# A four-layer hybrid decoder trunk: the tile layer orders each engine's instructions by its timeline model

## The chip, the cores and the metric

The kernel runs on one core of a Trainium2 chip. A core has five engines with an instruction stream each: PE (matrix products and transposes), DVE (vector work), ACT (activations and casts), POOL, and SP, which here only issues transfers. Semaphores make an engine wait for another's result; within a stream the order is fixed when the kernel is built. The metric is the device time of one execution in microseconds (us); less is better.

## The reference

A residual stream x of 256 tokens and 1024 features passes four layers in float32. Each layer has a token mixer, a cross-attention to 256 memory tokens and an MLP, and after each of the three a layer norm:

```python
for i in range(DEPTH):                      # DEPTH = 4
    # mixer i mod 3: 0 convolution module, 1 dilated attention, 2 RWKV-7
    x = layer_norm(DEEPNORM_ALPHA * x + mixer(x), ...)
    x = layer_norm(DEEPNORM_ALPHA * x + cross_attention(x, mem), ...)   # 4 heads of 256
    x = layer_norm(DEEPNORM_ALPHA * x + relu(x @ w1) ** 2 @ w2, ...)    # 1024 -> 4096 -> 1024
```

This sketch shortens the reference's code: the layers' mixers are thus convolution, dilated attention, RWKV-7 and convolution again.

## The kernel before

**Tiling.** x lies in SBUF as two tiles of 128 tokens by 1024 features. In the orders shown below they are named x_81 (tokens 0 to 127) and x_82 (tokens 128 to 255); the profile calls both x. A matrix product needs x transposed (features on partitions) and, to keep the precision of float32, in two parts, a rounded high part and the remainder: `xth` and `xtl`. `transposes` (L209, L213) turns four blocks of 128 x 128 on PE into one PSUM tile `psT`, and `split` (L151 to L153) casts it to the high part on ACT and subtracts to the low part on DVE.

**Weights.** Each chunk of 512 KB is loaded raw to `ws` (L137, three buffers), cast by ACT to its high part `wh` (L138) and subtracted by DVE, or POOL in one stretch, to its low part `wl` (L139); `wh` and `wl` have nine buffers each. A product is then three matmuls: high by high, high by low, low by high. `gemm_tok` (L156, matmul at L171) makes a product for one token tile with the 512 columns of a PSUM tile at a time; `gemm_feat` (L183) and `gemm_unit` (L195) make products for all tokens.

**The boundary between two sub-layers.** `project` (L280) runs the output product of a sub-layer for the first token tile, then its norm, then the product for the second tile and its norm. `norm` (L260) adds the product to x (L269) and takes statistics (L270) for each half, aggregates them (L271), works out 1 / sqrt(variance) with single-column steps on DVE (`rsqrt`, L238 to L245), then does a subtraction and scaling (L275) and a second scaling and shift (L276) for each half. Its end writes the transposes of the new x into the next sub-layer's `xth` and `xtl`. The next sub-layer's first product can start on the first token tile as soon as its parts are there. The MLP's first units (`first_rows`, L198) are made for one token tile and then for the other.

**What sets the order.** The mixers' work is interleaved in the program by generators (`merge`, with paces at L43 to L52). But the order in which the program names the operations is not yet that of the engines: the tile layer sorts each engine's instructions by its own model of when they can run, within what the data and the buffers allow, and places the semaphores to fit. With `tile.TileContext(nc)` (in `kernel`) it does so in its default way.

**Stages.** In the profiled execution (us from the start): convolution 0 to 190, cross-attention to 270, MLP to 457; dilated attention 457 to 765, cross-attention to 850, MLP to 1014; RWKV 1014 to 1355, cross-attention to 1445, MLP to 1605; convolution 1605 to 1780, cross-attention to 1862, MLP to 2045, last norm to 2056. The memory's keys and values (`kv_unit`) are made inside the mixers' stretches. In the dilated mixer a query or key unit is 24 matmuls (L648), and each pair of heads has scores, a softmax on DVE and ACT (L727 to L736), transposes of its result (copied at L750) and value products. In the convolution, taps are summed on PE and on DVE (L528); in the RWKV tail ACT copies the scan's parts (L1091).

Of the kernel before, what the change touches and what calls it, by code (L numbers as in the profile page):

```python
# [5 lines left out]

# [4 lines left out]

F32 = mybir.dt.float32
F32R = mybir.dt.float32r
# [11 lines left out]
DEPTH = 4  # L25
# [1271 lines left out]


@with_exitstack
def tile_trunk(ctx: ExitStack, tc: tile.TileContext, t: dict, out: bass.AP, stop: int = 99, layers=tuple(range(DEPTH))):  # L1300
    nc = tc.nc
    k = Trunk(ctx, tc, t)
    for i in range(NT):
        nc.sync.dma_start(k.x[i], t["x"][0, i * P:(i + 1) * P, :])
    xt = k.xt()
    for i in range(NT):
        k.to_xt(xt, k.x[i], i, layers[0] % 3 == 1)
    n = 0
    kv = {}
    done = False  # L1310
    fill = []

    def memory(ls, spare):

        mt = k.mem_t(spare=spare)
        for l in ls:
            kv[l] = k.kv_alloc()
        return [lambda l=l, u=u: k.kv_unit(l, kv[l], u, mt) for l in ls for u in range(8)]

    def staged(l):  # L1320

        mt = k.mem_t(spare=True)
        st = k.dr.tile([8, P, 512], F32, name="kvst")

        def last(us):
            kv[l] = k.kv_alloc()
            k.kv_load(kv[l], [u for u in range(8) if u not in us], st)
            for u in us:
                k.kv_unit(l, kv[l], u, mt)

        return [lambda u=u: k.kv_unit(l, None, u, mt, st) for u in range(8)] + [lambda: last(())]

    for i, layer in enumerate(layers):
        if layer % 3 == 0 and not fill:
            fill = memory((0, 1) if layer == 0 else (layer,), layer > 0)
        elif layer % 3 == 2 and not fill:
            fill = staged(layer)
        for part in ("mix", "xattn", "mlp"):
            if n >= stop:
                break  # L1340
            n += 1
            last = layer == DEPTH - 1 and part == "mlp"
            xo = None if last else k.xt()
            if part == "mix" and layer % 3 == 0:
                k.conv(layer, layer // 3, xt, xo, fill)
                fill = []
            elif part == "mix" and layer % 3 == 1:
                k.dilated(layer, layer // 3, xt, xo)
            elif part == "mix":
                k.rwkv(layer, layer // 3, xt, xo, fill)  # L1350
                fill = []
            elif part == "xattn":
                if layer not in kv:
                    with tc.tile_pool(name="kvp", bufs=1) as kvp:
                        mt = k.mem_t(kvp)
                        kv[layer] = k.kv_alloc()
                        for u in range(8):
                            k.kv_unit(layer, kv[layer], u, mt)
                k.xattn(layer, kv[layer], xt, xo)
            else:  # L1360
                nx = layers[i + 1] if i + 1 < len(layers) else None
                if nx == 3:
                    fill = memory((3,), True)
                elif nx == 2:
                    fill = staged(2)
                k.mlp(layer, xt, xo, nx is not None and nx % 3 == 1)
                for _ in range(2 if nx == 2 else 0):
                    fill.pop(0)()
            xt = xo
    for i in range(NT):  # L1370
        for j in range(2):
            nc.sync.dma_start(out[0, i * P:(i + 1) * P, j * 512:(j + 1) * 512], k.x[i][:, j * 512:(j + 1) * 512])
# [29 lines left out]
```

## Time and profile before

| What | Before |
|---|---|
| Time, median of 3 runs | 2058.87 us (2056.86 to 2062.66) |
| Time of the profiled execution | 2057.95 us |
| Span of the profiled execution, first to last instruction | 2056.2 us |
| Mean granted TensorE clock | 0.972 |
| ACT busy | 996.1 us (48%) |
| Traffic with HBM | 315.67 MB read, 6.88 MB written, 157 GB/s over the span |

A row of the timeline reads: start in us, duration in us, engine, line, operation, output and inputs, shapes, and how many equal instructions stand together. Square brackets hold the engine's idle time ahead of the row and what ended it. In a list of waits, a row names who waited for whom, the sum in us, the number of times, and the longest. In a row of windows stand the stretch, its length, the busy time and number of instructions of PE, PEld, DVE, ACT and POOL, the granted TensorE clock, the busy share of the DMA engines and GB/s.

### The profile page before, as it was taken

What the parts mean: (1) busy time and instruction counts of PE and PEld (TensorE: products, weight loads), DVE (VectorE), ACT (ScalarE), POOL (GpSimd) and SP (SyncE); (2) the same over time, 40 slices, a digit from 0 to 9 for tenths busy, and PEclk for the clock granted to TensorE, in tenths of its full rate; (3) what the DMA queues carried; (4) which work ended last, traced back from release to release, by engine and by line L of the source; (5) the groups of instructions that cost most, each with busy time, mean ns of one, the idle gap of its engine ahead of it and who ended that gap; (6) DMA issues with size and microseconds to landing.
All of it is one profiled execution on the core that took longest, in us unless ns stands there. A gap on an engine that the chain in (4) does not pass through costs nothing.

```text
span 2056.2 us, 33010 instructions
## 1 busy us (share of the span) xinstructions
PE 1944.8 (95%) x13027; PEld 1716.0 (83%) x13027; DVE 1302.7 (63%) x2524; ACT 996.1 (48%) x1551; POOL 264.9 (13%) x160
## 2 busy tenths in 40 slices
PE   7999999998999999999999989989999898999998
PEld 7998779977999977798888777767898787878996
DVE  3986675454555564755575767776554499667544
ACT  4546445543554533555345634333555355545552
POOL 6960000000000000000011312100000663000000
PEclk9999999998999999999999989999999999999999
DMA  7644447656656533576655334344666441445662
GB/s 228 195 154 145 146 147 232 186 163 186 169 147 175 155 117 112 188 221 186 181 160 169 102 103 118 113 138 129 198 199 188 160 144 52 138 139 179 213 188 78
DMA packets 259739, 325.75 MB, mean 158 GB/s; under 512 B 25701, under 2 KB 219965, under 8 KB 259584
## 3 DMA queue, kind: packets, MB, share of 16 engines
q1 hardware_dynamic: 258432, 322.59, 50.8%
q8 instruction: 102, 1.67, 0.3%
q10 hardware_dynamic: 1152, 1.05, 0.2%
q14 instruction: 53, 0.43, 0.1%
HBM read 315.67 MB, written 6.88 MB: 157 GB/s over the span
## 4 chain that ended last, share of the span: by engine, by line
PE 68%; DVE 15%; DMA 6%; ACT 5%; issue 4%; POOL 1%; SPq 0%; DVEq 0%; ACTq 0%; POOLq 0%
PE psA L171 25%; PE psB L183 19%; PE psB L648 7%; PE psB L195 6%; DVE g L528 3%; DVE wl L139 3%; PE psT L213 3%; ACT wh L138 2%; DMA ws<-in_m_w_dram 2%; PE psB L367 2%; POOL wl L139 1%; DMA ws<-in_x_w_out_dram 1%; DVE x L269 1%; DVE bnst L270 1%; DMA ws<-in_x_w_kv_dram 1%
## 5 line engine op out<-in xcount | busy, mean ns | idle before, releaser
L138 ACT CAST wh<-ws 128x1024 fp32r<-128x1024 f32 x546 | 571.4, 1050 | 664.5 <-PE psA L171 167.0
L139 DVE TENSOR_TENSOR wl<-ws,wh 128x1024 fp32r<-128x1024 f32 (+1 forms) x462 | 568.7, 1234 | 421.4 <-ACT wh L138 418.5
L183 PE MATMUL psB<-xth,wh 128*128 128x256 f32 x1280 | 369.1, 289 | 9.4 <-ACT xth L152 3.7
L183 PE MATMUL psB<-xth,wl 128*128 128x256 f32 x1280 | 367.0, 287 | 7.7 <-DVE wl L139 7.7
L183 PE MATMUL psB<-xtl,wh 128*128 128x256 f32 x1280 | 366.6, 286 | 0.0
L183 PEld LDWEIGHTS psB<-xth,wh 128*128 128x128 f32 x1280 | 249.8, 195 | 14.0 <-ACT xth L152 4.1
L139 POOL TENSOR_TENSOR wl<-ws,wh 128x1024 fp32r<-128x1024 f32 x84 | 211.0, 2536 | 380.9 <-ACT wh L138 372.7
L183 PEld LDWEIGHTS psB<-xth,wl 128*128 128x128 f32 x1280 | 249.5, 195 | 8.9 <-DVE wl L139 8.6
L183 PEld LDWEIGHTS psB<-xtl,wh 128*128 128x128 f32 x1280 | 249.7, 195 | 2.3 <-issue 0.2
L171 PE MATMUL psA<-wh,xth 128*128 128x512 f32 x496 | 180.2, 406 | 3.5 <-ACT xth L152 3.0
L171 PE MATMUL psA<-wl,xth 128*128 128x512 f32 x496 | 177.1, 400 | 0.0
L171 PE MATMUL psA<-wh,xtl 128*128 128x512 f32 x496 | 175.9, 399 | 0.0
L171 PE MATMUL psA<-wh,hth 128*128 128x512 f32 x512 | 163.7, 396 | 0.0
L171 PE MATMUL psA<-wh,htl 128*128 128x512 f32 x512 | 163.3, 395 | 0.0
L171 PE MATMUL psA<-wl,hth 128*128 128x512 f32 x512 | 162.3, 393 | 0.0
L528 DVE SCALAR_TENSOR_TENSOR psA<-chp,ccols,psA 128x256 f32<-128x256 f32 x280 | 119.1, 481 | 3.0 <-PE psA L512 0.4
L171 PEld LDWEIGHTS psA<-wh,xth 128*128 128x128 f32 x496 | 94.8, 193 | 25.2 <-ACT xth L152 7.1
L171 PEld LDWEIGHTS psA<-wl,hth 128*128 128x128 f32 x512 | 96.5, 188 | 22.9
L171 PEld LDWEIGHTS psA<-wh,htl 128*128 128x128 f32 x512 | 96.2, 188 | 22.0
L895 POOL MEMSET rH<- 128x512 f32 x1 | 0.5, 528 | 869.6 <-DVE bnst L270 869.6
L171 PEld LDWEIGHTS psA<-wl,xth 128*128 128x128 f32 x496 | 94.9, 192 | 19.0
L171 PEld LDWEIGHTS psA<-wh,xtl 128*128 128x128 f32 x496 | 94.6, 191 | 18.9 <-DVE xtl L153 0.2
(326 smaller groups left out, 3568.2 us busy)
## 6 DMA issues: line engine op xcount, KB each, us to landing
ws<-in_m_w_dram SPq DMA_DIRECT2D x256, 512.0 KB
ws<-in_b_w_qkv_dram SPq DMA_DIRECT2D x72, 512.0 KB
ws<-in_x_w_kv_dram SPq DMA_DIRECT2D x64, 512.0 KB
ws<-in_a_w_in_dram SPq DMA_DIRECT2D x32, 512.0 KB
ws<-in_x_w_q_dram SPq DMA_DIRECT2D x32, 512.0 KB
ws<-in_x_w_out_dram SPq DMA_DIRECT2D x32, 512.0 KB
ws<-in_c_w_rkv_dram SPq DMA_DIRECT2D x24, 512.0 KB
ws<-in_a_w_out_dram SPq DMA_DIRECT2D x16, 512.0 KB
```

What stands on the lines that cost most here:

```text
L138: nc.scalar.copy(out=h[:rows], in_=f[:rows])
L139: self.lo_eng.tensor_tensor(l[:rows], f[:rows], h.bitcast(F32)[:rows], op=OP.subtract)
L171: nc.tensor.matmul(ps[j], l, r[:, j * 512:(j + 1) * 512], start=first and k == 0 and i == 0, stop=last and k == n - 1 and i == 2)
L183: nc.tensor.matmul(ps[:, c * S + toks.start:c * S + toks.stop], l, r, start=k == 0 and i == 0, stop=k == KC - 1 and i == 2)
L195: nc.tensor.matmul(ps[:, m * 256:(m + 1) * 256], l, r[:, k % 4, :], start=k == 0 and i == 0, stop=k == KC - 1 and i == 2)
L213: self.pe_last = self.nc.tensor.transpose(pt[:, i * P:(i + 1) * P], b, self.ident).ins
L269: v.scalar_tensor_tensor(xs, xs, ALPHA, ps[j], op0=OP.mult, op1=OP.add)
L270: v.bn_stats(st[:, j, :], xs)
L367: nc.tensor.matmul(op[:, c * S:(c + 1) * S], vt[:, m, (2 * h + c) * P:(2 * h + c + 1) * P], pT[:, m, :], start=m == 0, stop=m == 1)
L528: v.scalar_tensor_tensor(dst[:, o], hp[:, c, k:k + S], dwc(k, cc), src[:, o], op0=OP.mult, op1=OP.add)
L648: nc.tensor.matmul(ps, l[:, k, :], r[:, k, :], start=k == 0 and i == 0, stop=k == KC - 1 and i == 2)
L895: nc.gpsimd.memset(H, 0.0)
```

## The change

The tile layer's context is now made with one more argument, which has it sort the instructions with its timeline model in place of its default one. A small class with the old name passes it on. Nothing else is touched; lines behind it have numbers higher by 10, so that L276 is L286 after.

```diff
-import concourse.tile as tile
+import concourse.tile as tiles
 from concourse import mybir
 from concourse._compat import with_exitstack
+class tile:
+    @staticmethod
+    def TileContext(nc):
+        return tiles.TileContext(nc, schedule_with_timeline_sim=True)
...
-def tile_trunk(ctx: ExitStack, tc: tile.TileContext, t: dict, out: bass.AP, stop: int = 99, layers=tuple(range(DEPTH))):
+def tile_trunk(ctx: ExitStack, tc: tiles.TileContext, t: dict, out: bass.AP, stop: int = 99, layers=tuple(range(DEPTH))):
```

Each engine has the same instructions before and after (PE 11863, DVE 2526, ACT 1497, SP 705 and POOL 165); their order differs. Some 950 stand elsewhere on PE, some 737 on DVE, 281 on ACT, 39 on SP and 5 on POOL. On SP, mostly one weight load stands ahead of the small loads of a norm's factors or of a tile of the memory. Two boundaries show what moves.

**From the first cross-attention to its MLP.** DVE before, from the last steps of x_81's rsqrt (L244, L245) to x_82's first statistics:

```order
L244 TENSOR_SCALAR rs_s<-bnrs,rs_a 128x1
L245 TENSOR_SCALAR bnrs<-rs_s,bnrs 128x1
L244 TENSOR_SCALAR rs_s<-bnrs,rs_a 128x1
L245 TENSOR_SCALAR bnrs<-rs_s,bnrs 128x1
L276 SCALAR_TENSOR_TENSOR x_81<-x_81,bnrs,lnb 128x512 x2
L139 TENSOR_TENSOR wl<-ws,wh 128x1024
L153 TENSOR_TENSOR xtl<-psT,xth 128x4x128
L269 SCALAR_TENSOR_TENSOR x_82<-x_82,psA 128x512
L153 TENSOR_TENSOR xtl<-psT,xth 128x4x128
L270 BN_STATS bnst<-x_82 128x6
```

DVE after, from the last of x_82's two adds (its first stands three rows above):

```order
L279 SCALAR_TENSOR_TENSOR x_82<-x_82,psA 128x512
L280 BN_STATS bnst<-x_82 128x6
L255 TENSOR_SCALAR bnrs<-rs_s,bnrs 128x1
L149 TENSOR_TENSOR wl<-ws,wh 128x1024
L280 BN_STATS bnst<-x_82 128x6
L254 TENSOR_SCALAR rs_s<-bnrs,rs_a 128x1
L149 TENSOR_TENSOR wl<-ws,wh 128x1024
L281 BN_AGGR bnmv<-bnst 128x2
L255 TENSOR_SCALAR bnrs<-rs_s,bnrs 128x1
L248 TENSOR_SCALAR rs_a<-bnmv 128x1
L285 SCALAR_TENSOR_TENSOR x_82<-x_82,bnmv,lng 128x512
L254 TENSOR_SCALAR rs_s<-bnrs,rs_a 128x1
```

x_81's last step (L276, now L286), which stood ahead of x_82's adds, has moved behind all of these rows: behind them follow L285 of x_82, L249, L255, L250 and L252, and then L286 of x_81. The last steps of x_81's rsqrt (L254, L255) are now between those of x_82's norm.

PE at the same boundary, before, at the end of the projection for x_82 (L171; `xth` here still holds the attention's output):

```order
L171 MATMUL psA<-wl,xth 128x512
L171 MATMUL psA<-wh,xtl 128x512
L213 MATMUL psT<-ident,x_81 128x128 x4
L171 MATMUL psA<-wh,xth 128x512
L213 MATMUL psT<-ident,x_81 128x128 x4
L171 MATMUL psA<-wl,xth 128x512
L171 MATMUL psA<-wh,xtl 128x512
L171 MATMUL psA<-wh,xth 128x512
```

PE after, from the last matmuls of that projection on:

```order
L181 MATMUL psA<-wl,xth 128x512
L181 MATMUL psA<-wh,xtl 128x512
L181 MATMUL psA<-wh,xth 128x512
L181 MATMUL psA<-wl,xth 128x512
L181 MATMUL psA<-wh,xtl 128x512
L223 MATMUL psT<-ident,x_81 128x128 x8
L181 MATMUL psA<-wh,xth 128x512 x2
L181 MATMUL psA<-wl,xth 128x512 x2
L181 MATMUL psA<-wh,xtl 128x512 x2
L181 MATMUL psA<-wh,xth 128x512 x2
```

The two groups of four transposes of x_81, which stood inside the projection of x_82, are now one group of eight behind its end, directly ahead of the MLP's first product (the rows with x2).

**From the dilated mixer to its cross-attention.** DVE before, from the last copy of a transposed softmax result (L750) through the norm of x_81:

```order
L750 COPY g_7839<-psT 128x512
L153 TENSOR_TENSOR xtl<-psA,xth 128x4x64
L269 SCALAR_TENSOR_TENSOR x_81<-x_81,psB 128x512 x2
L270 BN_STATS bnst<-x_81 128x6 x2
L139 TENSOR_TENSOR wl<-ws,wh 128x1024
L271 BN_AGGR bnmv<-bnst 128x2
L139 TENSOR_TENSOR wl<-ws,wh 128x1024
L238 TENSOR_SCALAR rs_a<-bnmv 128x1
L275 SCALAR_TENSOR_TENSOR x_81<-x_81,bnmv,lng 128x512
L239 TENSOR_SCALAR rs_i<-rs_a 128x1
L275 SCALAR_TENSOR_TENSOR x_81<-x_81,bnmv,lng 128x512
L240 TENSOR_SCALAR bnrs<-rs_i 128x1
```

DVE after, from the same copy (now L760):

```order
L760 COPY g_7839<-psT 128x512
L149 TENSOR_TENSOR wl<-ws,wh 128x1024 x2
L163 TENSOR_TENSOR xtl<-psA,xth 128x4x64
L149 TENSOR_TENSOR wl<-ws,wh 128x1024 x3
L279 SCALAR_TENSOR_TENSOR x_81<-x_81,psB 128x512 x2
L280 BN_STATS bnst<-x_81 128x6
L149 TENSOR_TENSOR wl<-ws,wh 128x1024
L280 BN_STATS bnst<-x_81 128x6
L279 SCALAR_TENSOR_TENSOR x_82<-x_82,psA 128x512 x2
L149 TENSOR_TENSOR wl<-ws,wh 128x1024
L281 BN_AGGR bnmv<-bnst 128x2
L149 TENSOR_TENSOR wl<-ws,wh 128x1024
```

Five weight subtracts (L149) now stand ahead of x_81's adds (L279), and x_82's adds have moved in ahead of x_81's aggregate (L281); x_81's last step, L286, comes 21 rows below the last row shown. The same mixing of the two norms stands behind the RWKV mixer; behind the convolutions only one subtract and one add of x_82 have moved ahead of x_81's last step.

## The prediction

> **What bounds the kernel now.** The first view is the page's list of busy times, then the chain that ended last, then the list of what PE waited for. Times are us.
>
> ```profile
> PE 1944.8 (95%) x13027; PEld 1716.0 (83%) x13027; DVE 1302.7 (63%) x2524; ACT 996.1 (48%) x1551; POOL 264.9 (13%) x160
> PE 68%; DVE 15%; DMA 6%; ACT 5%; issue 4%; POOL 1%; SPq 0%; DVEq 0%; ACTq 0%; POOLq 0%
> PE psT L213 <- DVE x L276: 27.9, 15, 6.5
> PE psT L213 <- DVE g L528: 12.5, 5, 5.3
> PE psT L213 <- DVE g L1184: 8.7, 2, 7.3
> PE psB L183 <- DVE wl L139: 7.7, 4, 4.2
> PE psT L213 <- DVE g L356: 6.7, 6, 1.5
> ```
>
> PE is busy for 95% of the span, and the same matmuls are issued before and after, so the time can fall at most by what PE idles, 2056.2 - 1944.8 = 111.4. It can rise without such a limit. The largest wait, 27.9 in 15 places, is of one kind: the eight transposes of a token tile (L213) wait for the last step of its layer norm (L276). These are the boundaries between sub-layers, where a serial chain runs from the last matmul over a norm on DVE, transposes on PE and a cast on ACT back to the next matmul. Before, the chain of the first token tile (x_81) mostly lies beside the matmuls of the second (x_82). What the change is worth is read there, since the order pieces above show that x_81's norm is now mixed with x_82's.
>
> **The change part by part: cross-attention to MLP, four times.** The first such boundary on PE, before:
>
> ```profile
> 266.89 0.39 PE L171 MATMUL psA<-wh,xtl 128*128 128x512 f32 x1
> 267.37 0.66 PE L213 MATMUL psT<-ident,x 128*128 128x128 f32 x4
> 268.12 0.63 PE L213 MATMUL psT<-ident,x 128*128 128x128 f32 x4
> 270.21 0.39 PE L171 MATMUL psA<-wh,xtl 128*128 128x512 f32 x1
> 278.61 0.39 PE L171 MATMUL psA<-wh,xth 128*128 128x512 f32 x1
> 281.11 0.39 PE L171 MATMUL psA<-wh,xtl 128*128 128x512 f32 x1
> 283.50 1.51 PE L213 MATMUL psT<-ident,x 128*128 128x128 f32 x8 [2.00 <-DVE x L276]
> 284.80 0.79 PE L171 MATMUL psA<-wh,xth 128*128 128x512 f32 x1
> ```
>
> From 278.61 to 281.11 are 11 steps: a matmul follows the other by 0.227 at full pace. x_81's transposes (267.37, 268.12) lie inside the output projection of x_82, whose last matmul is at 270.21; the MLP's first matmul comes 0.23 after it. By the order after, all eight stand behind that last matmul, and on DVE 18 rows stand from x_82's second add, which needs that matmul, to the first half of x_81's L276. Their durations before:
>
> ```profile
> 273.08 0.67 DVE L269 SCALAR_TENSOR_TENSOR x<-x,psA 128x512 f32<-128x512 f32 x1
> 274.80 0.69 DVE L270 BATCH_NORM_STATS2 bnst<-x 128x6 f32<-128x512 f32 x1
> 275.40 1.21 DVE L139 TENSOR_TENSOR wl<-ws,wh 128x1024 fp32r<-128x1024 f32 x1
> 276.53 0.20 DVE L271 BATCH_NORM_AGGREGATE bnmv<-bnst 128x2 f32<-128x12 f32 x1
> 277.74 0.14 DVE L238 TENSOR_SCALAR rs_a<-bnmv 128x1 f32<-128x1 f32 x1
> 277.81 0.74 DVE L275 SCALAR_TENSOR_TENSOR x<-x,bnmv,lng 128x512 f32<-128x512 f32 x1
> 280.93 0.27 DVE L244 TENSOR_SCALAR rs_s<-bnrs,rs_a 128x1 f32<-128x1 f32 x1
> 281.23 0.21 DVE L245 TENSOR_SCALAR bnrs<-rs_s,bnrs 128x1 f32<-128x1 f32 x1
> 282.60 1.42 DVE L276 SCALAR_TENSOR_TENSOR x<-x,bnrs,lnb 128x512 f32<-128x512 f32 x2
> ```
>
> One add 0.67, two statistics 1.38, two weight subtracts 2.42, one aggregate 0.20, two L275 1.48, two L244 0.54, three L245 0.63, four single-column steps like L238 0.56, half of L276 0.71: 8.6. The rows lie over each other by about 0.07 (277.74 + 0.14 against 277.81), which over 18 rows takes up to 1.2: 7.4 to 8.6. Behind it come four transposes, 0.66, and the cast of their result on ACT:
>
> ```profile
> 266.85 1.05 ACT L138 CAST wh<-ws 128x1024 fp32r<-128x1024 f32 x1 [3.23 <-DMA ws<-in_m_w_dram]
> 268.06 0.59 ACT L152 CAST xth<-psT 128x512 fp32r<-128x512 f32 x1 [0.17 <-PE psT L213]
> ```
>
> With 0.66 and 0.59 the MLP's first matmul comes 8.7 to 9.9 after the last matmul, where it came 0.23 after it. I take the middle, 9.3: a loss of 9.1. Three things are to be set against it. The transposes no longer stretch the projection: from 266.89 to 270.21 are 3.32 for 10 steps of 0.227, so 1.05 is regained. The old wait for x_82 goes: its L276 stands nine rows behind x_81's now, while PE works on x_81's MLP. From 281.11 to 284.80 are 3.69; with the step of 0.23 and about 0.9 for the transposes themselves taken off, 2.6 is regained. And a clock that falls after a wait:
>
> ```profile
> 283.00:289.00 6.00, 5.47 (x24) 4.41 (x25) 2.82 (x5) 2.34 (x6) 0.00 (x0) 0.72 0.57 193
> ```
>
> Six us at a granted clock of 0.72 lose 6.00 x 0.28 = 1.7 after a wait of only 2.00. That loss goes at x_82's transposes and comes back at x_81's: nothing in sum. The two subtracts among the 18 need casts of weights that may not have come (the cast above waited 3.23 for its DMA): 0 to 2.5, taken as 1.2. Sum: 9.1 - 1.05 - 2.6 + 1.2 = **+6.7** (4.8 to 8.5), four times **+26.8**.
>
> The Trainium skill ("TensorE: Matmul & The Clock Gate", "Part 1: The HAM clock gate (the "warmup" mystery)") states that the clock halves only after an idle window of about 3.4 us. By that rule the old wait of 2.00 need not have cost anything in clock, only the new one of some 9 would, and the sum would be 4 x 1.7 = 6.8 higher, an estimate from the page's rule. The row of 0.72 speaks against it, and the row decides.
>
> **Mixer to cross-attention.** After a conv mixer (layers 0 and 3) only a subtract (1.21) and an add (0.67) of x_82 have moved ahead of x_81's last step: the next gemm starts 1.6 later by these less their overlap. Its low half (xtl) stands behind two subtracts, a statistic and an add more, 3.8, of which the high-half matmuls hide an uncertain part. From 1.6 to 5.4, taken as 3.7 each: **+7.4**.
>
> After the dilated mixer it is much more:
>
> ```profile
> 747.14 1.39 DVE L269 SCALAR_TENSOR_TENSOR x<-x,psB 128x512 f32<-128x512 f32 x2 [0.59 <-PE psB L171]
> 756.85 1.05 ACT L138 CAST wh<-ws 128x1024 fp32r<-128x1024 f32 x1 [1.42 <-DMA ws<-in_x_w_q_dram]
> 759.81 1.29 PE L213 MATMUL psT<-ident,x 128*128 128x128 f32 x8 [1.80 <-DVE x L276]
> 762.77 1.22 PE L171 MATMUL psA<-wh,xth 128*128 128x512 f32 x2 [1.67 <-ACT xth L152]
> ```
>
> x_81's adds ran at 747.14 and could start its norm 10 us ahead of the end. Now five weight subtracts stand ahead of them, and the fifth needs the cast of 756.85, which waited for its DMA: it ends at 757.90 + 1.21 = 759.1. From x_81's adds to the first half of its last step stand four adds 2.8, four statistics 2.8, three subtracts 3.6, two aggregates 0.4, four L275 3.0, eight single columns 1.1, six L244 1.6, five L245 1.05 and 0.7: 17.0, or 14.5 less overlaps. With 1.25 for transposes and cast the query gemm starts at 774.9 to 777.4, not at 762.77: 12.1 to 14.6, taken as **+13.4**. PE has nothing else in its order there.
>
> After the RWKV mixer x_81's last step stands behind the same 18 rows as at the MLP, 8.7 to 9.9 with transposes and cast:
>
> ```profile
> 1353.09 0.47 PE L171 MATMUL psA<-wh,xtl 128*128 128x512 f32 x1
> 1354.01 0.73 PE L171 MATMUL psA<-wh,xth 128*128 128x512 f32 x2
> ```
>
> Before it was 0.92: +7.8 to 9.0, and here a fallen clock is new, 1.7: **+10.1** (7.8 to 10.7).
>
> **MLP to mixer, three times.** Here PE waited already:
>
> ```profile
> 461.39 1.78 PE L213 MATMUL psT<-ident,x 128*128 128x128 f32 x8 [3.81 <-DVE x L276]
> 469.67 1.94 PE L213 MATMUL psT<-ident,x 128*128 128x128 f32 x8 [6.50 <-DVE x L276]
> ```
>
> No weight subtract can stand long in these chains that did not before; steps of x_82 cost x_81 0 to 2 and give it back at x_82. Taken as 1 each: **+3**.
>
> **Inside the mixers.** The rows on which this rests:
>
> ```profile
> 584.50 0.28 PE L648 MATMUL psB<-xtl,wh 128*128 128x256 f32 x1
> 585.21 0.42 DVE L736 TENSOR_SCALAR svs<-svs,dden 128x384 f32<-128x384 f32 x1
> 1320.32 0.36 ACT L1091 COPY rW<-psB 64x256 f32<-64x256 f32 x1 [0.67 <-PE psB L1090]
> 1332.06 1.05 ACT L138 CAST wh<-ws 128x1024 fp32r<-128x1024 f32 x1 [2.35 <-PE psB L1119]
> ```
>
> In the dilated mixer the transposes of each pair of heads come one query unit or so earlier: the softmax row ends at 585.63, where PE would come to them at 584.5, up to 1.1 lost for each of 8 pairs, and about as much regained at the value products: -10 to +9, taken as 0. In the RWKV tail two weight casts (1332.06) now stand ahead of copies of the scan (1320.32). If they still need a buffer that comes free at 1332.06, the copies lose up to 1333.11 - 1320.32 = 12.8; if the buffer is free by then, nothing. Taken as 0, since PE's freeing matmuls may move with them. The second conv mixer is bound by DVE, whose subtracts move ahead of its last taps: -4 to +6, taken as +1. On the SP queue one weight load moves ahead of small loads at a few places by single us; covered by its three buffers: 0.
>
> **Sum:** 26.8 + 7.4 + 13.4 + 10.1 + 3 + 1 = 61.7. The profiled execution took 2057.95 (span 2056.2 and 1.75 around it), 0.92 under the median of the runs. 2057.95 + 61.7 = 2119.7: I predict **2120**.
>
> **Rivals.** *Waits inside the mixers go as well.* The new order brings results and transposes nearer to each other, and the waits for L528, L1184, L139 and L356 are 12.5 + 8.7 + 7.7 + 6.7 = 35.6. If all went, 61.7 - 35.6 = 26: 2084. For it: the order moves transposes there. Against it: on DVE the steps that they wait for depend on matmuls that have not moved.
>
> *Faster.* The same 35.6 go, and the eleven boundaries cost little, because DVE, with 37% of its time free, reaches them early and x_82's adds find their sums ready. It decides when a boundary costs under 35.6 / 11 = 3.2. At the mean old wait of 27.9 / 15 = 1.9 each it is 20.5 - 35.6 = -15: 2043. Against it: x_82's last add cannot run ahead of the last matmul, and 18 rows behind it are 8.6 whatever DVE did earlier.
>
> *Larger loss.* The uncertain interiors go to their upper ends: +9 in the dilated mixer, +12.8 in the RWKV tail, 5 more in the conv mixer: 61.7 + 27 = 89: 2147. It decides when the casts in the RWKV tail still wait for the matmul of 1332.06.
>
> *No change.* Losses at boundaries are covered by regained waits just so: 2058. Only a chance meeting of large terms gives it.
>
> **How the numbers follow.** Forecast (2105 to 2140) 0.62, larger loss 0.13, partly regained 0.12, faster 0.09, no change 0.04. The range 2080 to 2155 holds the first three and leaves out the last two and some tails. A change of 0.3%, about 6 us, is what a measurement of this kernel can tell from none: faster 0.09, same 0.04, slower 0.87.
>
> **What would show it.** In the changed kernel's list of PE's waits, the wait of L223 for x (L286) should grow from 27.9 to about 70 to 80, with one of over 10 behind the dilated mixer, one of 6 to 8 behind the RWKV mixer and four of 6 to 8 ahead of the MLPs; busy time of PE, DVE and ACT should stay but for the clock. The waits for x_82's tile ahead of the MLP's second half should be gone. I am wrong if the MLP's first matmul stands within 4 of the last projection matmul, or if the waits in the mixers change by more than 15.

## The result, and the profile after

| What | Before | After |
|---|---|---|
| Time, median of 4 runs each | 2060.40 us | 2156.34 us |
| Ratio, with its 95% interval | 1 | 1.0488 (1.0468 to 1.0509) |
| Time of the profiled execution | 2057.95 us | 2157.15 us |
| Span | 2056.2 us | 2155.4 us |
| Mean granted TensorE clock | 0.972 | 0.945 |

The change makes the kernel slower, by 99.2 us in the profiled executions. 61.7 had been forecast: the direction was right, the size too small, and the time lies just outside the range of 2080 to 2155. The page's busy times, its chain, and the list of what PE waited for, of the changed kernel:

```profile
PE 1955.2 (91%) x13027; PEld 1737.1 (81%) x13027; DVE 1302.7 (60%) x2524; ACT 999.6 (46%) x1551; POOL 267.0 (12%) x160
PE 73%; DVE 12%; DMA 6%; ACT 4%; issue 3%; POOL 1%; SPq 0%; DVEq 0%; ACTq 0%; POOLq 0%
PE psT L223 <- DVE x L286: 81.0, 12, 12.3
PE psT L223 <- DVE g L538: 24.7, 3, 14.4
PE psT L223 <- DVE g L366: 24.7, 4, 6.9
PE psT L223 <- DVE g L1194: 4.8, 1, 4.8
PE psB L193 <- DVE wl L149: 3.4, 2, 3.2
```

DVE is busy for 1302.7 as before, ACT 3.5 longer. PE idles 2155.4 - 1955.2 = 200.2, where it idled 111.4: 88.8 of the 99.2. The other 10.4 is PE's own busy time for the same matmuls; the mean granted clock is lower, 0.945 against 0.972, but no run shows that this is all of it. Three rows carry most of the new idle time: the wait for x_81's and x_82's norm rose by 53.1, that for the taps of the convolution (L538, before L528) by 12.2, that for the softmax of the cross-attention (L366, before L356) by 18.0.

Where in the program the time went is seen when the PE timeline is cut at the first query matmul of each cross-attention and at the first matmul of each MLP. A stretch "cross-attention" reaches from the one to the other, and so holds the boundary to the MLP; the next reaches from the MLP's first matmul to the next query matmul. The cuts are found by counting matmuls.

| Stretch, us | Before | After | Difference |
|---|---|---|---|
| up to the first query matmul | 203.4 | 205.5 | +2.1 |
| four cross-attentions | 67.1, 70.7, 69.4, 67.1 | 86.0, 83.8, 84.3, 86.0 | +65.8 |
| first MLP and dilated mixer | 492.3 | 492.6 | +0.3 |
| second MLP and RWKV mixer | 520.6 | 533.9 | +13.3 |
| third MLP and second convolution | 371.0 | 388.4 | +17.4 |
| last MLP and norm | 194.7 | 194.9 | +0.2 |

Two thirds of the loss lie in the cross-attentions and at the boundary behind them: 48.8 of the 65.8 between the projection's last matmul and the MLP's first (0.23 each before, 12.2 to 12.6 now), and 14.0 between the scores and the projection's last matmul, where the softmax stands.

That boundary, in the timeline of the changed kernel; first PE, then DVE, then ACT, at the place where the prediction worked out its first sum:

```profile
279.08 0.39 PE L181 MATMUL psA<-wh,xtl 128*128 128x512 f32 x1
289.76 1.94 PE L223 MATMUL psT<-ident,x 128*128 128x128 f32 x8 [10.29 <-DVE x L286]
291.52 1.22 PE L181 MATMUL psA<-wh,xth 128*128 128x512 f32 x2
292.54 1.05 PE L181 MATMUL psA<-wl,xth 128*128 128x512 f32 x2
293.39 1.05 PE L181 MATMUL psA<-wh,xtl 128*128 128x512 f32 x2
```

```profile
281.06 1.23 DVE L149 TENSOR_TENSOR wl<-ws,wh 128x1024 fp32r<-128x1024 f32 x1 [0.59 <-ACT wh L148]
282.39 0.68 DVE L279 SCALAR_TENSOR_TENSOR x<-x,psA 128x512 f32<-128x512 f32 x1
283.70 1.22 DVE L149 TENSOR_TENSOR wl<-ws,wh 128x1024 fp32r<-128x1024 f32 x1
285.60 1.22 DVE L149 TENSOR_TENSOR wl<-ws,wh 128x1024 fp32r<-128x1024 f32 x1
288.86 1.41 DVE L286 SCALAR_TENSOR_TENSOR x<-x,bnrs,lnb 128x512 f32<-128x512 f32 x2
```

```profile
281.61 1.05 ACT L148 CAST wh<-ws 128x1024 fp32r<-128x1024 f32 x1 [0.58 <-DMA ws<-in_m_w_dram]
284.32 1.05 ACT L148 CAST wh<-ws 128x1024 fp32r<-128x1024 f32 x1 [1.67 <-DMA ws<-in_m_w_dram]
```

From the projection's last matmul (279.08) to the MLP's first (291.52) are 12.44, where 9.3 and 1.2 for late weights had been forecast. The chain from x_82's second add to the end of the first half of x_81's last step, 282.39 to 289.57, is 7.2, just under the 7.4 to 8.6 worked out. But the add started 3.3 after the start of the matmul that it needs. Ahead of it in DVE's queue stood a subtract that waited 0.59 for a cast, which waited for a weight, and then took 1.23 itself. The cast that waited until 284.32 held nothing: its subtract (285.60) started without idle time ahead of it.

### The profile page after: what moved, and what is told of

It reads as the page before. It is cut to its first block, busy times and chain, and to the rows that moved or that the text cites. A ratio compares the mean times of both kernels' runs of the same rounds, so it can differ in the third digit from the quotient of the medians.

```text
span 2155.4 us, 33048 instructions
## 1 busy us (share of the span) xinstructions
PE 1955.2 (91%) x13027; PEld 1737.1 (81%) x13027; DVE 1302.7 (60%) x2524; ACT 999.6 (46%) x1551; POOL 267.0 (12%) x160
## 3 DMA queue, kind: packets, MB, share of 16 engines
q1 hardware_dynamic: 258432, 322.59, 48.8%
## 4 chain that ended last, share of the span: by engine, by line
PE 73%; DVE 12%; DMA 6%; ACT 4%; issue 3%; POOL 1%; SPq 0%; DVEq 0%; ACTq 0%; POOLq 0%
PE psA L181 27%; PE psB L193 20%; PE psB L205 7%; PE psB L658 6%; PE psT L223 3%; DVE wl L149 3%; DMA ws<-in_m_w_dram 2%; ACT wh L148 2%; DVE g L538 2%; PE psB L377 2%; PE psA L522 1%; PE psA L205 1%; DVE x L285 1%; DVE bnst L280 1%; DVE x L286 1%
## 5 line engine op out<-in xcount | busy, mean ns | idle before, releaser
L149 DVE TENSOR_TENSOR wl<-ws,wh 128x1024 fp32r<-128x1024 f32 (+1 forms) x462 | 568.3, 1233 | 482.5 <-ACT wh L148 464.9
L149 POOL TENSOR_TENSOR wl<-ws,wh 128x1024 fp32r<-128x1024 f32 x84 | 210.6, 2527 | 392.8 <-DMA ws<-in_a_w_in_dram 290.1
L538 DVE SCALAR_TENSOR_TENSOR psA<-chp,ccols,psA 128x256 f32<-128x256 f32 x280 | 121.1, 483 | 3.0
L223 PE MATMUL psT<-ident,x 128*128 128x128 f32 x192 | 37.2, 352 | 88.0 <-DVE x L286 81.0
L181 PEld LDWEIGHTS psA<-wl,hth 128*128 128x128 f32 x512 | 96.5, 188 | 22.9
```

The lines of the kernel that those rows point to most:

```text
L149: self.lo_eng.tensor_tensor(l[:rows], f[:rows], h.bitcast(F32)[:rows], op=OP.subtract)
L181: nc.tensor.matmul(ps[j], l, r[:, j * 512:(j + 1) * 512], start=first and k == 0 and i == 0, stop=last and k == n - 1 and i == 2)
L223: self.pe_last = self.nc.tensor.transpose(pt[:, i * P:(i + 1) * P], b, self.ident).ins
L538: v.scalar_tensor_tensor(dst[:, o], hp[:, c, k:k + S], dwc(k, cc), src[:, o], op0=OP.mult, op1=OP.add)
```

## Two theories

**A, late weight subtracts.** The timeline model places the subtracts of the next sub-layer's weights ahead of the steps that end a stretch. On the chip their weights come later than that: at this boundary four of the seven casts wait for their DMAs. A subtract that waits at the head of DVE's queue holds everything behind it.

**B, mixed norms.** x_81's last norm step waits because x_82's steps, which need the last matmul of the projection, stand ahead of it; the subtracts cost only their own time.

The experiments on the order keep every instruction; they only hold some behind others on the same engine, with `issue_after`, which fixes the order in the queue and adds no wait for a result. Their edits are shown shortened, with comments added. The kernel before ran at 2051 to 2053 in the medians of these runs; the changed kernel is compared through its ratio of 1.0488. Stretches are compared with the profiled execution of the changed kernel.

### Norms unmixed, subtracts left in place

```diff
+        with self.tc.issue_after(self.n0) if t else nullcontext():   # n0: x_81's last norm step
             for j in range(2):
                 xs = x[:, j * 512:(j + 1) * 512]
                 v.scalar_tensor_tensor(xs, xs, ALPHA, ps[j], op0=OP.mult, op1=OP.add)
                 v.bn_stats(st[:, j, :], xs)
```

> The changed kernel, but on DVE the adds of x_82 are held behind the last norm step of x_81 at every boundary; the weight subtracts stay where the timeline model put them, so seven of them still stand ahead of x_81's last step at the boundary to the MLP. Theory A (late weight subtracts: a subtract at the head of DVE's queue waits for the cast of a weight that has not come, and holds all behind it): x_81's step still waits for the seventh subtract, whose cast ended at 285.4 in the changed kernel; the waits for x of 10.1 to 10.5 ahead of the four MLPs stay above 6, and the time gains no more than 20, about 2135 to 2156. Theory B (mixed norms: x_81's last step waits because x_82's steps stand ahead of it): the step comes free before the last matmul, these four waits fall below 3, and the time falls by 30 to 50, to about 2105 to 2125.

Ratio 1.0408 (1.0347 to 1.0469), 2135.7 us, where the changed kernel's 1.0488 would be 2151: a gain of 15. The list of PE's waits, and DVE at the same boundary, of this kernel:

```profile
PE psT L225 <- DVE x L289: 67.8, 11, 8.1
```

```profile
286.61 1.23 DVE L151 TENSOR_TENSOR wl<-ws,wh 128x1024 fp32r<-128x1024 f32 x1 [0.58 <-ACT wh L150]
288.00 1.42 DVE L289 SCALAR_TENSOR_TENSOR x<-x,bnrs,lnb 128x512 f32<-128x512 f32 x2
```

x_81's last step, now ahead of x_82's adds, still starts only at 288.00, right behind the seventh subtract, which waited for its cast. The four waits ahead of the MLPs are 7.9, 8.0, 8.1 and 7.7. Theory A said above 6, B below 3. B alone falls as the account of this kernel.

How the subtracts hold the step is not quite as A has it. From x_81's second add to its last step are 15.6 here, and 5.2 in the next kernel, which has no subtract between them. Of the 10.4 more, DVE idles 2.6 for casts; the rest is the seven subtracts' own time (8.6, with overlaps). In the changed kernel the seven take 8.6 too, and DVE idles 1.5 to 1.8 for their casts at each of the four boundaries to an MLP. The place of the subtracts in the queue costs more than the lateness of their weights.

### Subtracts behind x_81's last step

```diff
+        late = self.gate is not None and self.lo_eng is nc.vector    # gate: x_81's last norm step
+        with self.tc.issue_after(self.gate) if late else nullcontext():
             self.lo_eng.tensor_tensor(l[:rows], f[:rows], h.bitcast(F32)[:rows], op=OP.subtract)
```

> The changed kernel, but the weight subtracts of the next sub-layer are held behind x_81's last norm step at every boundary. Theory A: the four waits ahead of the MLPs fall from about 10.3 to below 3 and those behind the dilated and the RWKV mixer (12.3 and 8.4) to below 4; the time falls by 40 to 55, to 2100 to 2116. Theory B: by itself this takes 2.4 of two subtracts out of each chain, so some 15 at most: 2140 or more, as long as x_82's adds stay ahead of x_81's last step.

Ratio 1.0460 (1.0392 to 1.0528), 2146.4 us. Ahead of the MLPs the wait for x_81 is gone, as A expected: each MLP's first matmul comes 1.5 after the projection's last. Behind the dilated mixer 7.8 is left, where A expected below 4. The four cross-attentions take 79.1, 74.9, 74.7 and 76.9, together 34.5 shorter. Yet the time hardly moved, as B had forecast (2140 or more). In the list of waits of this kernel stand:

```profile
PE psT L228 <- DVE x L291: 54.1, 14, 10.6
PE psA L186 <- DVE wl L154: 6.1, 11, 0.8
PE psA L186 <- DVE xtl L168: 5.6, 6, 1.0
```

The subtracts now come after x_81 and within x_82's norm, whose waits are the new ones: 1.6 to 3.7 ahead of the MLPs' second token tile, 10.6 behind the first MLP. The three stretches from MLP to query are 9.7, 5.6 and 6.1 longer than in the changed kernel, the last MLP 7.2. The loads moved too. A load needs one of the three `ws` buffers, which its subtract sets free; the fourth load of the first MLP's weights goes out at 280.44, right behind the first subtract that is released (279.15, 1.22 long). In the kernel with the norms unmixed the fourth went out at 244.28. So the hold is real, but holding all subtracts back only moves the loss. With this order x_82's adds also fell behind x_81's last step, so this run alone cannot tell A from B.

### Both, with three subtracts free

This kernel has both edits, and the first three subtracts of a sub-layer may still pass ahead.

> The changed kernel with x_82's adds held behind x_81's last norm step and only the first three weight subtracts of the next sub-layer free to pass ahead of it. If both causes add up (mixed norms cost 6.2 in each cross-attention when alone, late subtracts the rest): the cross-attention stretches fall from 84 to 87 to 72 to 76, and since three subtracts are done early the MLP does not pay as when all were held back: it stays within 2 of the changed kernel's from the MLP's first matmul to the next cross-attention. Time 35 to 50 below the changed kernel, ratio 1.023 to 1.031. If the subtracts are merely moved into the MLP, the ratio stays above 1.037.

Ratio 1.0293 (1.0271 to 1.0315), 2113.4 us; the cross-attentions are 72.7, 76.4, 76.3 and 73.1, 41.6 shorter in sum than in the changed kernel, and the first MLP's stretch is 490.1, 2.5 shorter. 40 us of the loss are thus the order of DVE at the boundaries; unmixing alone had brought the cross-attentions 12.6, so the subtracts make the greater part of it. The 40 are a net gain: between the first MLP and the dilated mixer the two waits for x grew from 8.1 and 2.4 to 1.1 and 15.8, since the held subtracts stand in x_82's norm there.

### The kernel before, with only the norms mixed

The rest of x_81's norm is traced behind x_82's adds, and held there:

```diff
+        if t:
+            self.rest(a.ins)       # a: x_82's second add
...
+        def rest(after):
+            with self.tc.issue_after(after) if after else nullcontext():
+                for j in range(2):
+                    xs = x[:, j * 512:(j + 1) * 512]
+                    v.scalar_tensor_tensor(xs, xs, rs, b[:, j * 512:(j + 1) * 512], op0=OP.mult, op1=OP.add)
+            if xt is not None:
+                self.to_xt(xt, x, t, classes)
```

> The kernel before, with its default order, but x_81's last norm step is held behind x_82's second add at every boundary, without any more subtracts ahead of it. Theory A: a boundary loses only x_81's step, four transposes and a cast behind the last matmul, some 2.6, less what the transposes no longer stretch in the projection, so 1 to 2 at each of eleven: 2070 to 2085. Theory B: each boundary loses about what the changed kernel lost there, 8 to 12: 2130 or more.

Ratio 1.0181 (1.0118 to 1.0244), 2089.2 us: 38 slower, between the two forecasts. Of it 22.9 lie in the cross-attentions (72.9, 75.3, 75.7, 73.3). Its list of waits, and PE and DVE at the first boundary to an MLP:

```profile
PE psT L213 <- DVE x L283: 47.4, 15, 6.3
274.29 0.39 PE L171 MATMUL psA<-wh,xtl 128*128 128x512 f32 x1
278.79 0.66 PE L213 MATMUL psT<-ident,x 128*128 128x128 f32 x4 [4.11 <-DVE x L283]
280.12 0.79 PE L171 MATMUL psA<-wh,xth 128*128 128x512 f32 x1 [0.68 <-DVE bnmv L273]
```

```profile
275.65 1.23 DVE L139 TENSOR_TENSOR wl<-ws,wh 128x1024 fp32r<-128x1024 f32 x1 [0.85 <-ACT wh L138]
277.40 0.67 DVE L269 SCALAR_TENSOR_TENSOR x<-x,psA 128x512 f32<-128x512 f32 x1
```

The MLP's first matmul comes 5.5 to 6.5 after the projection's last, more than the loss of 1 to 2 that A expected and less than the 8 to 12 of B. But this kernel is not free of late weights: a subtract stands between x_82's two adds here too, DVE idles 0.5 to 1.4 for its cast, and the second add starts 2.8 to 3.8 after the matmul. From that add to the MLP's first matmul are 2.7, which is A's 2.6 for mixing. So no run shows the mixing without a subtract, and the 38 are the price of both together. The prices of the two faults do not add: with both in place, taking one away leaves the other to set the end.

### The softmax first

The same hold, with the last softmax step of the second head as gate, on the subtracts that are traced behind it: those of the output weights, and of the MLP weights that had moved ahead of it.

> The changed kernel, but in the cross-attention the subtracts of the output weights are held behind the softmax of the second head. Theory A: the four waits of PE for the softmax (24.7 in sum) fall to below 10 and the time by 12 to 20, to 2136 to 2144. Rival (the softmax is late because scores, table load and exponentials on ACT are late): waits stay above 18, time within 6 of 2156.

Ratio 1.0381 (1.0302 to 1.0461), 2130.3 us. In the list of waits the softmax falls from 24.7 to 6.3, and the cross-attentions are 18.0 shorter (81.6, 78.9, 80.6, 81.0); the time gained 21, a little more than the 12 to 20 expected. The waits for x ahead of the MLPs rose to between 11.2 and 12.2, though in three of these four chains DVE hardly idles for a cast (0.05 at most): the order alone can make that wait. The two rows:

```profile
PE psT L226 <- DVE x L289: 83.7, 12, 12.2
PE psT L226 <- DVE g L369: 6.3, 8, 1.5
```

What was wrong in the changed kernel is seen in its DVE timeline, beside ACT and PE:

```profile
238.22 1.23 DVE L149 TENSOR_TENSOR wl<-ws,wh 128x1024 fp32r<-128x1024 f32 x1 [0.79 <-ACT wh L148]
239.37 0.68 DVE L357 TENSOR_REDUCE mx<-psA 128x2 f32<-128x512 f32 x1
240.92 1.23 DVE L149 TENSOR_TENSOR wl<-ws,wh 128x1024 fp32r<-128x1024 f32 x1 [0.87 <-ACT wh L148]
242.07 0.68 DVE L357 TENSOR_REDUCE mx<-psA 128x2 f32<-128x512 f32 x1
```

```profile
239.85 1.05 ACT L148 CAST wh<-ws 128x1024 fp32r<-128x1024 f32 x1 [1.65 <-DMA ws<-in_m_w_dram]
```

```profile
246.41 1.94 PE L223 MATMUL psT<-ident,g 128*128 128x128 f32 x8 [6.94 <-DVE g L366]
```

The reduces that start a softmax (L357) stand behind subtracts that wait for their casts, 0.79 and 0.87, and take 1.23 each; the second is for a weight of the MLP. As at the boundary, subtracts stand ahead of the step that PE needs, and their own time is more than the waits.

### All on DVE, and the transposes

The next kernel has unmixed norms with three subtracts free, the softmax first, and the taps first (below); the one after it also holds the last six matmuls of x_82's projection behind x_81's transposes on PE.

> All three edits on DVE at once (norms unmixed with three subtracts free, softmax first, taps first). If the three are separate losses, their gains add: 40 for the boundaries, 18 for the softmax, 12 for the taps, so 70 of 96, ratio 1.010 to 1.018. If they are one loss that moves from place to place, the gain is below 45, ratio above 1.025.

> As the last, and x_81's transposes held ahead of the last six matmuls of x_82's projection on PE. Transposes and cast are then beside matmuls again: 1 to 2 less at each of eight boundaries, ratio 1.000 to 1.010. If the interior of the dilated mixer keeps the 7 that it gained, it may come out under the kernel before, ratio 0.996 or more. If the position of the transposes does not matter, the ratio equals that of the last run.

Ratios 1.0286 (1.0262 to 1.0310) and 1.0232 (1.0209 to 1.0256). The gains of the first do not add: it is no faster than the kernel without the softmax first (1.0293). The four cross-attentions sum to 291.8, 6.7 less than there, but the rest is 3 longer. The wait for the softmax fell from 18.0 to 6.3, that for x rose from 33.4 to 40.7, and PE waits for the low half of x right behind the MLP's first matmuls:

```profile
PE psA L186 <- DVE xtl L168: 22.7, 8, 3.9
PE psT L228 <- DVE g L375: 6.3, 8, 1.5
279.18 1.05 PE L186 MATMUL psA<-wh,xtl 128*128 128x512 f32 x2 [3.87 <-DVE xtl L168]
```

The first row was 15.9 in the kernel without the softmax edit. Holding single steps repairs a place and makes the next one late. The transposes' place was worth 11 by the ratios, within the 8 to 16 expected of it, though the expected ratio, 1.000 to 1.010, was missed; 3.5 of it lie in the cross-attentions (288.3). The second kernel still has 532.9 in the RWKV stretch and 386.0 in the convolution's, 12.3 and 15.0 more than before, although its query matmuls come 0.2 to 0.5 after the projections. Part of the wait there has only moved ahead of the six matmuls that are held: the RWKV mixer's output product takes 70.6 from its first matmul to its last, 64.7 in the changed kernel.

### The convolution: a miss, and half a hit

I had put the taps' lateness down to subtracts as well: three that waited 2.9, 1.0 and 4.8 stood ahead of the last taps. The same hold, with the last tap as gate:

> The changed kernel, but in the second convolution the subtracts of the output weights are held behind the last tap. Late weight subtracts (three that waited 2.9, 1.0 and 4.8 for their casts stood ahead of the last 34 taps): PE's waits for the taps fall from 24.7 to 12 or less, as before the change, and the time by 10 to 15. Rival (the taps are late because DVE is simply full there): waits stay above 20 and the time within 6 of the changed kernel's, which is 1.047 to 1.049 of the kernel before.

Ratio 1.0499 (1.0475 to 1.0524): nothing gained, and theory A falls for this place. So does the rival of a full DVE, since DVE idles there. DVE and PE in this kernel:

```profile
1807.88 0.87 DVE L541 SCALAR_TENSOR_TENSOR g<-chp,ccols,psA 128x256 f32<-128x256 f32 x2 [12.26 <-PE psA L525]
1808.67 12.75 DVE L541 SCALAR_TENSOR_TENSOR g<-chp,ccols,g 128x256 f32<-128x256 f32 x32
```

```profile
1821.17 1.21 PE L226 MATMUL psT<-ident,g 128*128 128x128 f32 x4 [13.28 <-DVE g L541]
```

DVE, without the subtracts, simply idles 12.26 for the sum of the taps that PE makes, and then PE idles 13.28 for DVE's 32 taps. On PE the last unit's 28 tap matmuls stood one by one between memory products: in the changed kernel they take 37.5, where they took 13.4. So the next kernel holds the memory products that are traced later behind the last tap:

```diff
+                with self.tc.issue_after(self.tap) if j and len(tapped) == 4 else nullcontext():
                     f()                # one unit of the memory's products
```

> The changed kernel, but in the second convolution the memory products on PE that are traced behind the last unit's PE taps are held behind the last of these taps. New theory for the convolution (the timeline model spread the last unit's 28 tap matmuls thinly between memory products, so that DVE idled 12.3 for their sum, and PE then idled 13 to 14 for DVE's 32 taps): PE's waits for the taps fall from 24.7 to 12 or less, the stretch from the third MLP to the last cross-attention falls from 388 to 372 to 378, and the time by 10 to 16. Rival (the sum is late because ACT makes the products late): the waits stay above 20 and the time within 6.

Ratio 1.0453 (1.0427 to 1.0478), 2145.5 us; the wait for the taps is 16.6, its longest 8.6, and the stretch 381.4, 7.0 shorter; the 28 taps take 12.7. The expected 12 or less, 372 to 378 and 10 to 16 were missed, and the interval overlaps the changed kernel's (1.0468 to 1.0509), so the time alone does not show the gain. The wait, down by 8.1, does: the order of the taps on PE is a cause, for some 7 of the 17 lost there. Of the other 10, some 4 are waits for taps still above the 12.5 before; the rest stays open.

### A version faster than both

Inside the dilated mixer the changed kernel had gained: from the mixer's first matmul to the end of the projection (471.4 to 757.8, and 490.6 to 770.1) 286.4 became 279.5. On PE its order put the three groups of four transposes of a softmax result between the query and key units, where before they stood together behind the last unit. The default order follows the program there, so the order in which the program names them was changed:

```diff
                 for _ in items(hp + 1):
                     step()
                     if soft:
                         soft.pop(0)()
-                values(hp, flips(), self.B())
+                    else:
+                        next(flip, None)      # one group of four transposes and its copy
+                for _ in flip:
+                    pass
+                values(hp, pts, self.B())
```

> The kernel before, default order, but in the dilated mixer the three groups of four transposes of a softmax result are traced between the query and key units, one behind each unit once the four softmaxes are done, as the timeline model placed them, not all behind the last unit. If this place is what gave the changed kernel 7 inside the dilated mixer, the stretch from the first MLP to the second cross-attention falls from 492 to 485 to 488 and the time by 4 to 7: ratio 0.9965 to 0.998. If the 7 came from elsewhere (scores, weights, the start of the mixer), the time is within 2 of the kernel before.

Ratio 0.9950 (0.9934 to 0.9966), 2041.9 us: faster than both kernels, by 10 than the one before, where 4 to 7 had been expected. The stretch of the first MLP and the dilated mixer is 478.8, 13.5 less than in the profiled execution before, 11.8 of it inside the mixer. There PE had idled only 2.1 before. On this kernel's page PE's busy time is 1934.4, 10.4 less than before at the same mean granted clock of 0.972, so that most of what was gained had been counted as busy there and stood in no list of waits:

```profile
PE 1934.4 (95%) x13027; PEld 1714.0 (84%) x13027; DVE 1303.7 (64%) x2524; ACT 995.3 (49%) x1551; POOL 265.9 (13%) x160
```

## Why the prediction was right in direction and too small

**Right.** The reading of the order: x_81's norm behind x_82's adds and behind subtracts, its transposes behind the projection. The forecast for PE's wait for x was 70 to 80, and it is 81.0; one above 10 behind the dilated mixer is there:

```profile
782.40 1.94 PE L223 MATMUL psT<-ident,x 128*128 128x128 f32 x8 [12.29 <-DVE x L286]
```

Behind the RWKV mixer it is 8.4, forecast 6 to 8. The waits for x_82 ahead of the MLPs' second half are gone, and "MLP to mixer" stayed small.

**A sign of being wrong came.** "If the waits in the mixers change by more than 15": the four that the first rival counts as such sum to 57.6 where they were 35.6 (32.9 and 28.9 without the softmax, which stands in the cross-attention). Two of them shrank as that rival had it (8.7 to 4.8, 7.7 to 3.4), but the taps and the softmax grew by 12.2 and 18.0, and with that the rival fell.

**The first term was too small: cross-attention to MLP, "+6.7, four times".** The chain was nearly right (7.2, where 7.4 to 8.6 stood). Wrong was to start it at the last matmul, with "0 to 2.5, taken as 1.2" for late weights: x_82's second add came 3.1 to 3.3 after that matmul, because a subtract stands ahead of each of x_82's two adds, and only 0.3 to 0.7 of this was idle time of DVE for a cast. Wrong was also "that loss goes at x_82's transposes and comes back at x_81's: nothing in sum". The six us from the new transposes on, in the changed kernel's row of windows:

```profile
289.70:295.70 6.00, 5.94 (x18) 4.91 (x19) 4.54 (x11) 1.17 (x2) 0.00 (x0) 0.52 0.31 102
```

At 0.52 they lose 2.9, where 1.7 was lost after the shorter wait before; from the transposes to the MLP's first matmul it took 1.76, not the 1.25 that I had put in for transposes and cast. Together 12.44 instead of 10.5 from matmul to matmul. The waits are 10.1 to 10.5 at all four, not 6 to 8; from the projection's last matmul to the MLP's first the four boundaries lost 48.8, where 41.2 had been put in (4 x 10.3), before what is regained. On the clock the Trainium skill ("TensorE: Matmul & The Clock Gate", "Part 1: The HAM clock gate (the "warmup" mystery)") says that the array needs about 3.4 us of sustained work to come back to full rate. Here the matmuls stand 0.42 apart until about 295.1, 3.6 after the MLP's first matmul and 5.3 after the first transposes. Counted from the matmul this agrees; no run shows whether the transposes count.

**A term was missing: the softmax inside the cross-attention.** The sum has no term for it; the only mention of L356 was as a wait that might go. It grew by 18.0, and the run with the softmax first gave back 18.0 in the cross-attentions. The same kind of row that I had weighed at the boundary, a subtract ahead of the step that PE waits for, stood there too.

**"The second conv mixer ... taken as +1".** It measured +16.9 from the mixer's first matmul to its last, far more than the +6 at the end of its range. I had looked at the subtracts ahead of the last taps; the experiment shows that holding them back gains nothing, and that the tap matmuls' places on PE cost some 7. "Bound by DVE" was wrong too: DVE idled 12.26 for PE's sum of the taps once the subtracts were held back.

**The RWKV mixer, "+10.1".** From the projection's last matmul to the query's first 0.92 became 10.52, +9.6: this term was right. The mixer itself lost 4.1 more, taken as 0. The new waits there are many and small, and no experiment took them apart.

**The dilated mixer, "+13.4" and inside it "-10 to +9, taken as 0".** From the last projection matmul's end to the query matmul 5.0 became 14.1, +9.1 rather than 13.4, and the inside gained 6.9. The stretch as a whole came out even. Behind the two convolutions 5.5 were lost, not 7.4. Had these three come out as forecast, the miss would have been larger by 13: that it was not is luck.

## What to carry to other kernels

When an order changes, go through every place where an engine waits at the end of a stretch, not only the boundaries: for each, count the time of all rows that now stand ahead of the awaited step, and look which of them need something from memory, with their arrival taken from the trace. Start the chain where its first row can start, not where its input is ready. Two faults at one place do not add, so a repair is worth what is left after the other; and a row that is held back may hold a buffer, and with it a load. An order that loses as a whole may still hold a piece worth keeping, and such a piece can be taken over by hand.

## What was not expected of the hardware

A wait of 10.29 left a granted clock of 0.52 over the next six us, one of 2.00 still 0.72: a wait of a fifth of the length still cost more than half as much clock (1.7 against 2.9). Length alone does not set it: after the 12.29 behind the dilated mixer it was 0.62. And holding x_81's last step behind x_82's second add, in the order before, cost 38 us in eleven boundaries, though it adds no work; a subtract between x_82's two adds had its part in that.
